# Sums of hi and lo parts for the token operands: VectorE instead of GpSimd

## The chip, the cores and the metric

The kernel runs on one core of a Trainium2 chip. The metric is the device time of one execution in microseconds (us), from the first to the last instruction and what lies around them; lower is better. The engines are TensorE (PE in the rows; PEld is its weight load), VectorE (DVE), ScalarE (ACT), GpSimd (POOL) and SyncE (SP), which issues nearly all DMA transfers here. Each engine takes its instructions strictly in the order in which they stand in its queue; semaphores order the engines among each other.

## The reference

One step of a diffusion backbone over 640 tokens (128 of a prompt, 512 samples) of 1024 features. The change touches the two feed-forward blocks that open and close the layer:

```python
def swiglu(h, w13, w2):
    a, b = jnp.split(h @ w13, 2, axis=-1)
    return (jax.nn.silu(a) * b) @ w2

def ffn_sublayer(x, norm_w, shift, scale, gate, w13, w2):
    return x + HALF_STEP * gate * swiglu(modulate(rms_norm(x, norm_w), shift, scale), w13, w2)
```

`w13` has 2 x 2816 columns, `w2` 2816 rows. Between the two blocks stand a gated delta-rule mixer and a windowed attention, which the change does not touch. All values are float32.

## The kernel before, in words

Tokens lie along the free axis, in two halves of 320 (`HT`); features lie on the partitions, in 8 tiles of 128 (`KD`). TensorE multiplies in a reduced format, so every operand is split exactly into a first part (hi) and a rest (lo), and a product takes three matmuls: hi x hi, hi x lo, lo x hi. For token operands the parts are the tiles `hh` and `hl`; for weights `wh`/`wl` (1024 columns) and `sh`/`sl` (512 columns, L128 on ScalarE and L132 on VectorE), made from `wraw`, which SyncE loads.

A feed-forward block (`ffn`) goes over 22 pairs of feature tiles f, in six rounds (`ROUNDS`); behind each round come its products with `w2`. The first three, f = 0, 1, 2 (`DIRECT`), are computed directly: a and b over all 8 k tiles, 48 matmuls each; then SiLU of a on ScalarE (L491), the multiplication with b on VectorE, which reads b from PSUM (L492, two instructions, one for each half), and the split of the result (L501 ScalarE, L502 VectorE). From f = 3 on `product_pair` computes a and b by seven products of quarters instead of eight, in the order p1, p6, p5, p7, two more into one large bank, p4, 12 matmuls each (L207). For these it needs differences of quarters of the weights, four GpSimd instructions (L577 to L580), and of the token operands.

The token operands of that kind are made once for each block, while TensorE does f = 1 and f = 2. `combined_operands` is called behind f = 1: for each of four k tiles (`KH`) it adds hi and lo of three quarters again (L536, GpSimd), takes three differences (L541, VectorE) and splits each (L544 ScalarE to `th`, L545 VectorE to `tl`). `last_operand` is called behind f = 2: for each of four tiles two such sums (L558, GpSimd), one difference (L562), and its split into the place of the quarter B12 of `hh`/`hl` (L563 ScalarE, L564 VectorE). This last operand, T4, is needed by p4 alone. So there are 12 + 8 sums in each block, 40 in the kernel.

What sets the order of the work: a tile scheduler puts each engine's instructions in a queue by its own estimates of when they are ready; the code's order is only its starting point. PSUM tiles called `aux` are four banks used in turn: a product of f = 2 takes the banks that the L492 of f = 1 and the modulation copies have to free, and p6 and p5 take those that the L492 of f = 2 frees. There are three `wraw` buffers, so a load of weights waits until the parts of an earlier one are made. In the first block the quarters of the modulation vectors are also computed in between (L277 load `araw` by SyncE, L281 TensorE, L290 and L292 VectorE).

```python
if f == 1:
    B = self.combined_operands(hs)
if f == DIRECT - 1:
    self.last_operand(hs, B)
```

Of the kernel before, what the change touches and what calls it, by code (L numbers as in the profile page):

```python
# [10 lines left out]
F32 = mybir.dt.float32  # L11
# [4 lines left out]
ALU = mybir.AluOpType  # L16
PSUM = bass.MemoryType.PSUM
DRAM = bass.MemoryType.DRAM
# [6 lines left out]
T = SEQ + DEC  # L25
# [70 lines left out]
# columns of a half (0: the prompt and the first 192 samples, 1: samples alone) by kind, 0 prompt, 1 sample  # L96
# [3 lines left out]
class Net:  # L100
# [9 lines left out]
    # ---------------------------------------------------------------- weights  # L110
# [8 lines left out]
    def parts(self, raw, small=False):  # L119
        """Exact split of float32 weights into two float32r parts."""  # L120
        nc = self.nc
        n = raw.shape[1]
        if small:
            hi, lo = (self.tile(self.phase, [P, n], F32R, tag, self.nsh) for tag in ("sh", "sl"))
        else:
            hi, lo = (self.tile(self.wpool, [P, KD * P], F32R, tag, self.nwh)[:, :n] for tag in ("wh", "wl"))
        with self.tc.high_priority(offset=0 if self.first_weights else 20):
            nc.scalar.copy(hi, raw)  # L128
            if self.first_weights:
                nc.gpsimd.tensor_tensor(lo, raw, hi.bitcast(F32), op=ALU.subtract)  # L130
            else:
                nc.vector.tensor_sub(lo, raw, hi.bitcast(F32))  # L132
        return hi, lo
# [10 lines left out]
    def product(self, w, xs, c0=0, split=None):  # L144
        """[128 features, tokens] = w^T x over the k tiles; operands come as exact parts. split: None for one
        view of both halves, otherwise a view of each half, in small tiles when true."""
        if split:
            hv = [self.aux_tile()[:, 0:HT] for _ in range(2)]
        else:
            ps = self.tile(self.big, [P, 2, 512], F32, "big", 2)  # L150
            hv = (ps[:, 0, 0:HT], ps[:, 1, 0:HT])
        if self.by_half:
            self.by_half -= 1
            self.accumulate(hv, w, xs, c0, (1,))
            self.accumulate(hv, w, xs, c0, (0,))
        else:
            self.accumulate(hv, w, xs, c0, (0, 1))
        return ps[:, :, 0:HT] if split is None else hv
# [26 lines left out]
    def products_by_half(self, ws, xs, done):  # L185
        """Several products with the second halves of all before the first ones; done(i, half, psum)."""
        for h in (1, 0):
            for i, w in enumerate(ws):
                if h:
                    ps = self.aux_tile()[:, 0:HT]  # L190
                else:
                    if i % 2 == 0:
                        both = self.tile(self.big, [P, 2, 512], F32, "big", 2)
                    ps = both[:, i % 2, 0:HT]
                self.accumulate({h: ps}, w, xs, 0, (h,))
                if h == 0 and i == len(ws) - 1:
                    yield
                done(i, h, ps)

    def products(self, ps, w, xs):  # L200
        """One half of the tokens and of the k tiles: ps (+)= w^T x."""
        nc = self.nc
        wh, wl = w
        n = len(xs)
        for k, (xh, xl) in enumerate(xs):
            for j, (wt, xt) in enumerate(((wh, xh), (wh, xl), (wl, xh))):
                nc.tensor.matmul(  # L207
                    ps,
                    lhsT=wt[:, k * P : (k + 1) * P],
                    rhs=xt,  # L210
                    start=(k == 0 and j == 0),
                    stop=(k == n - 1 and j == 2),
                )

    # ---------------------------------------------------------------- small helpers
    def rsqrt(self, y, x):
        """y = x ** -0.5, elementwise on a small tile."""
# [14 lines left out]
    # ---------------------------------------------------------------- setup  # L232
# [37 lines left out]
    def modulation(self, m):  # L270
        """One of the nine modulation vectors, features on partitions, for prompt and sample; a generator with one
        quarter of the k tiles in each step."""
# [34 lines left out]
    def modulation_part(self, m0, g):  # L307
        """Two feature tiles (2 g, 2 g + 1) of the modulation vectors m0 and m0 + 1."""
# [35 lines left out]
    def scale_columns(self, m, at, t, d0=0, n=KD):  # L344
        """norm weight * (1 + scale) as per-partition columns."""
# [9 lines left out]
    def token_rstd(self, ss):  # L355
        """[128 tokens, n] sums of squares -> rstd."""
# [8 lines left out]
    def half_rstd(self, acc, h):  # L365
        """rstd of the tokens of one half, from squares [128, 2, 320]: columns of 128 tokens that start at 0, 128
        and 192, so the last one overlaps."""
# [8 lines left out]
    def half_rows(self, columns):  # L376
        """(column of 128 tokens, first token, tokens, place) -> a row [320] on each partition."""
# [19 lines left out]
    def modulated(self, hs, X, rb, A, m_shift, h, ds):  # L397
        """x * rstd * A + shift of one half as two exact parts, for the feature tiles ds."""
# [23 lines left out]
    def next_operands(self, last, X, A, m_shift):  # L422
        """Operands of the next products; last: the generator that makes the last tiles of X."""
# [14 lines left out]
    def add_square(self, acc, x, first):  # L438
        """acc (+)= x * x for one half."""
# [15 lines left out]
    def residual(self, ws, xs, X, gate, tail, weight=None):  # L455
        """X += gate * product, with the squares of the sums gathered in acc; the last tiles go by halves."""
# [18 lines left out]
    # ---------------------------------------------------------------- ffn  # L475
    def ffn(self, hs, X, gate, w13, w2, gpool, between=None, first=(), weight=None):
        """X += gate * swiglu(h); squares of the result are gathered into acc."""
# [49 lines left out]
    def combined_operands(self, hs):  # L527
        """The parts of the sums of quarters of h = [[B11, B12], [B21, B22]] (k halves by token halves) that
        product_pair takes: T1 = B12 - B11, T2 = B22 - T1, T3 = B22 - B12."""
        nc = self.nc  # L530
        T = [[], [], []]
        for d in range(KH):
            v = []
            for k, h in ((d, 1), (d, 0), (d + KH, 1)):
                t = self.tile(self.phase, [P, HT], F32, "ht", self.nht)
                nc.gpsimd.tensor_tensor(t, *(x[:, h, :].bitcast(F32) for x in hs[k]), op=ALU.add)  # L536
# [13 lines left out]
    def last_operand(self, hs, B):  # L550
        """B21 - T2, in the place of B12."""
        nc = self.nc
        B["T4"] = []
        for d in range(KH):
            v = []
            for x in (B["21"][d], B["T2"][d]):
                t = self.tile(self.phase, [P, HT], F32, "ht", self.nht)
                nc.gpsimd.tensor_tensor(t, x[0].bitcast(F32), x[1].bitcast(F32), op=ALU.add)  # L558
# [8 lines left out]
    def product_pair(self, w, ca, cb, B, s):  # L567
        """s = silu(a) * b for the products a, b of two tiles of features with h, by seven products of quarters
        in place of eight (Winograd's form of Strassen's product)."""
# [42 lines left out]
    # ---------------------------------------------------------------- attention  # L612
    def rope(self, x, pool):
        """Rotates x [128 = 2 heads, samples] in place."""
# [9 lines left out]
    def attention_inputs(self, pool, tmp, hs):  # L624
        """Parts of the keys (columns: prompt, cache, samples, cache again), values with tokens on partitions,
        queries."""
# [57 lines left out]
    def query_parts(self, pool, qall, c, r):  # L684
        """Exact parts of the queries of one r and of blocks c and c + 1: for each head of the two, the first
        part on its own partitions and the second on the other head's."""
# [16 lines left out]
    def attention_block(self, pool, c, kd, kl, vt, qall):  # L703
        """One block of 128 queries; a generator, so that blocks can be interleaved."""
# [75 lines left out]
    # ---------------------------------------------------------------- mixer A inputs  # L780
# [69 lines left out]
    def conv(self, pool, ps, tile_index, out):  # L850
        """Centred short convolution and silu of one 128-channel tile; out [128, 640]."""
# [25 lines left out]
    def to_token_major(self, src, dst):  # L877
        """src [128, 640] -> dst[:, c, :]."""
# [8 lines left out]
    def mixer_a_inputs(self, tmp):  # L887
        """Generators, one for each head and kind, that make the inputs of the delta rule."""
# [47 lines left out]
    def feed(self, primary, late, units, hs, rounds):  # L936
        """Products of the units spread over the rounds of another generator, each followed by its unit's own
        work, in pieces."""
# [40 lines left out]
    # ---------------------------------------------------------------- delta rule  # L979
    def delta_front(self, pool, scan_pool, c, units):  # L980
        """L, I + L and the intra-chunk weights of both directions of one chunk."""
# [54 lines left out]
    def delta_prep(self, pool, scan_pool, c, units):  # L1036
        """(I + L)^-T of both directions of one chunk."""
# [50 lines left out]
    def delta_step(self, pool, c, dr, units, S, zero, update, first):  # L1088
        """One chunk of the scan; S [128 dk, 4, 128 dv] is updated in place."""
# [61 lines left out]
    def interleave(self, active, pending, width):  # L1151
        """Emits generators round robin, `width` at a time; a generator may start more."""
# [70 lines left out]
    def delta_output(self, pool, c):  # L1223
        """o * rstd * onorm * silu(z) of a finished chunk, in the place of o; the query's own norm enters
        through eps alone."""
# [30 lines left out]
    def z_gate(self, pool, h, ps):  # L1256
        """silu(z) * onorm of one head, kept in DRAM until the end of the scan."""
# [9 lines left out]
    def after(self, k):  # L1267
        """Where step k of a product has its place: behind the modulation parts at the start, spread over the
        products of the delta rule while it runs."""
# [20 lines left out]
    def operand(self, z, tiles):  # L1290
        """Exact split of z [128, 2, 320] into two float32r parts, in the tiles given."""
# [92 lines left out]
    def output(self, pool, X, acc):  # L1384
        """Final norm, back to tokens on partitions; X comes with the weight of the norm in it."""
# [22 lines left out]
    # ---------------------------------------------------------------- everything  # L1408
    def build(self):
# [12 lines left out]
        with (  # L1422
# [8 lines left out]
            # first half step  # L1431
# [57 lines left out]
            # mixer  # L1489
            with ExitStack() as right:  # L1490
# [67 lines left out]
                with pool("x2") as xpool:  # L1558
# [11 lines left out]
                    # second half step  # L1570
# [40 lines left out]
```

## Time and profile before

| | |
|---|---|
| median of 3 runs | 1606.71 us (1606.54 to 1610.02) |
| span of the profiled execution | 1605.0 us |
| instructions | 28532 |
| TensorE busy | 1542.7 us, 96% |
| VectorE busy | 1100.8 us, 69% |
| ScalarE busy | 664.5 us, 41% |
| GpSimd busy | 368.7 us, 23% |
| chain that ended last, by engine | TensorE 80%, VectorE 11%, issue 3%, ScalarE, DMA and GpSimd 2% each |

The profile is of one execution and lists no separate time for it: its span stands beside the runs' times, 1.7 us under their median. Busy time is the share in which an engine works at all; it is an average over stages. The chain that ended last is followed back from the last instruction, at each step to what released it. "issue" is time in which an engine waited for nothing that the profile shows. Idle time of an engine costs something only where TensorE, or whatever ends last, waits for it.

### The profile page before, as it was taken

Reading aid. Unit: us, or ns where it says so; the run is one execution under the profiler, and the core shown is the slowest. Engines: PE = TensorE matmul, PEld = TensorE weight load, DVE = VectorE, ACT = ScalarE, POOL = GpSimd, SP = SyncE. Lnnn points to the kernel's source line nnn. Section 1 sums busy time; section 2 is a strip of 40 time slices with the busy share of each in tenths; the row PEclk is TensorE's granted clock in tenths of the full one; section 3 lists DMA queues with packets and bytes.
Section 4 is the critical chain, followed back from the end, with each engine's and each line's share of the span. In section 5 each row is a group of like instructions: output and inputs, shape, how many; then the busy total and the mean of one; then the engine's idle time right before and its main releaser. Section 6 shows DMA issues by size and latency. Waiting matters only on the chain.

```text
span 1605.0 us, 28532 instructions
## 1 busy us (share of the span) xinstructions
PE 1542.7 (96%) x11242; PEld 1457.5 (91%) x11242; DVE 1100.8 (69%) x2241; ACT 664.5 (41%) x1234; POOL 368.7 (23%) x306
## 2 busy tenths in 40 slices
PE   6989999999999899999899999999879999999998
PEld 4889999999999798788899999899879999999997
DVE  5866666668576768886665655764796766767675
ACT  4433323324243646554455544333542424334244
POOL 3632131222220220100221213000352232331310
PEclk8999999999999999999999999999999999999999
DMA  9444434545325241214533324545022322323122
GB/s 329 148 144 141 159 123 143 163 152 168 119 82 137 82 138 44 65 40 134 161 117 94 98 78 127 158 127 167 14 79 79 92 66 66 106 66 106 53 79 66
DMA packets 221296, 181.17 MB, mean 113 GB/s; under 512 B 16160, under 2 KB 198621, under 8 KB 221163
## 3 DMA queue, kind: packets, MB, share of 16 engines
q1 hardware_dynamic: 220907, 179.29, 36.3%
q8 instruction: 89, 1.46, 0.4%
q14 instruction: 44, 0.36, 0.1%
q0 software_dynamic: 256, 0.06, 0.0%
HBM read 161.59 MB, written 16.42 MB: 111 GB/s over the span
## 4 chain that ended last, share of the span: by engine, by line
PE 80%; DVE 11%; issue 3%; ACT 2%; DMA 2%; POOL 2%; SPq 0%; POOLq 0%; DVEq 0%; ACTq 0%
PE big L177 29%; PE aux L207 20%; PE aux L177 9%; PE aux L164 9%; PE big L207 8%; DVE ht L404 1%; DVE wl L132 1%; PE aux L281 1%; DVE ht L541 1%; DVE sl L132 1%; PE aux L161 1%; DMA wraw<-ffn_w 1%; DVE x L451 1%; DVE tl L545 1%; DVE cacc L867 1%
## 5 line engine op out<-in xcount | busy, mean ns | idle before, releaser
L128 ACT CAST wh<-wraw 128x1024 fp32r<-128x1024 f32 (+1 forms) x147 | 150.8, 1026 | 266.3 <-PE aux L177 90.1
L132 DVE TENSOR_TENSOR wl<-wraw,wh 128x1024 fp32r<-128x1024 f32 (+1 forms) x145 | 181.8, 1254 | 85.7 <-ACT wh L128 84.4
L177 PE MATMUL big<-hl,wh 128*128 128x320 f32 x768 | 194.7, 321 | 6.9 <-POOL hl L411 4.3
L177 PE MATMUL big<-hh,wh 128*128 128x320 f32 x768 | 187.8, 319 | 4.0 <-ACT hh L1293 1.8
L177 PE MATMUL big<-hh,wl 128*128 128x320 f32 x768 | 187.8, 315 | 0.7 <-DVE wl L132 0.7
L128 ACT CAST sh<-ss 128x512 fp32r<-128x512 f32 x152 | 92.5, 620 | 185.1 <-POOL ss L578 93.6
L577 POOL TENSOR_TENSOR ss<-wraw 128x512 f32<-128x512 f32 x38 | 53.9, 1418 | 485.0 <-DMA wraw<-ffn_w 337.3
L132 DVE TENSOR_TENSOR sl<-ss,sh 128x512 fp32r<-128x512 f32 x152 | 132.3, 880 | 46.8 <-ACT sh L128 45.9
L207 PE MATMUL aux<-th,sh 128*128 128x320 f32 x456 | 141.3, 310 | 3.2 <-DVE s L492 2.8
L177 PEld LDWEIGHTS big<-hl,wh 128*128 128x128 f32 x768 | 131.4, 190 | 13.0 <-POOL hl L411 7.0
L207 PE MATMUL aux<-tl,sh 128*128 128x320 f32 x456 | 141.1, 309 | 0.0
L207 PE MATMUL aux<-th,sl 128*128 128x320 f32 x456 | 140.8, 309 | 0.0
L177 PEld LDWEIGHTS big<-hh,wh 128*128 128x128 f32 x768 | 129.0, 190 | 9.8 <-issue 3.1
L177 PEld LDWEIGHTS big<-hh,wl 128*128 128x128 f32 x768 | 131.1, 190 | 5.8 <-issue 4.6
L451 DVE SCALAR_TENSOR_TENSOR x<-big,gate,x 128x128 f32<-128x128 f32 (+2 forms) x181 | 67.4, 422 | 34.6 <-PE big L177 34.3
L177 PE MATMUL big<-gh,wh 128*128 128x320 f32 x352 | 88.7, 313 | 1.1 <-ACT gh L501 1.1
L207 PEld LDWEIGHTS aux<-th,sh 128*128 128x128 f32 x456 | 85.8, 188 | 4.0 <-DVE s L492 3.0
L177 PE MATMUL big<-gl,wh 128*128 128x320 f32 x352 | 87.6, 310 | 0.0
L177 PE MATMUL big<-gh,wl 128*128 128x320 f32 x352 | 87.0, 308 | 0.0
L207 PEld LDWEIGHTS aux<-tl,sh 128*128 128x128 f32 x456 | 85.7, 188 | 0.0
L207 PEld LDWEIGHTS aux<-th,sl 128*128 128x128 f32 x456 | 85.7, 188 | 0.0
L1055 DVE TENSOR_TENSOR P<-aux,lv 128x512 f16<-128x512 f32 x70 | 48.2, 688 | 49.1 <-PE aux L164 49.1
(373 smaller groups left out, 4014.0 us busy)
## 6 DMA issues: line engine op xcount, KB each, us to landing
wraw<-ffn_w SPq DMA_DIRECT2D x116, 512.0 KB, 3.9
araw<-ada_w SPq DMA_DIRECT2D x56, 512.0 KB, 5.8
wraw<-w_in SPq DMA_DIRECT2D x35, 512.0 KB, 3.8
araw<-ada_w SPq DMA_DIRECT2D x32, 256.0 KB, 6.5
wraw<-ffn_w SPq DMA_DIRECT2D x16, 384.0 KB, 3.1
gd<-stage SPq DMA_DIRECT2D x16, 320.0 KB, 2.9
wraw<-w_out SPq DMA_DIRECT2D x8, 512.0 KB, 4.3
xd<-x SPq DMA_DIRECT2D x8, 320.0 KB, 2.2
```

What stands on the lines that cost most here:

```text
L128: nc.scalar.copy(hi, raw)
L132: nc.vector.tensor_sub(lo, raw, hi.bitcast(F32))
L161: self.marks.append(self.nc.tensor.transpose(*args))
L164: self.marks.append(self.nc.tensor.matmul(*args, **kw))
L177: self.nc.tensor.matmul(ps[h], lhsT=wt[:, k, c0 : c0 + P], rhs=xt[:, h, :], start=(k == 0 and j == 0), stop=(k == len(xs) - 1 and j == 2),)
L207: nc.tensor.matmul(ps, lhsT=wt[:, k * P : (k + 1) * P], rhs=xt, start=(k == 0 and j == 0), stop=(k == n - 1 and j == 2),)
L281: nc.tensor.matmul(ps[32 * g : 32 * g + 32], lhsT=self.s32[:, k, :], rhs=raw[:, g * 256 : (g + 1) * 256], start=(k % 2 == 0), stop=(k % 2 ...
L404: mark = nc.vector.scalar_tensor_tensor(t[:, cols], X[d][:, h, cols], A[:, d, v : v + 1], rb[:, cols], op0=ALU.mult, op1=ALU.mult)
L451: nc.vector.scalar_tensor_tensor(X[:, h, cols], ps[:, cols], gate[:, d, v : v + 1], X[:, h, cols], op0=ALU.mult, op1=ALU.add)
L541: nc.vector.tensor_sub(f[i], v[x], v[y] if y < 3 else f[0])
L577: nc.gpsimd.tensor_tensor(f[0], b[:, :n], b[:, n:], op=ALU.add)
L1055: nc.vector.tensor_tensor(P16, p1, mask, op=ALU.mult)
```

## The change

The engine of two instructions changes; what they compute and which tiles they read and write stays. (Comments and docstrings were also dropped, without moving a line.)

```diff
@@ combined_operands
             for k, h in ((d, 1), (d, 0), (d + KH, 1)):
                 t = self.tile(self.phase, [P, HT], F32, "ht", self.nht)
-                nc.gpsimd.tensor_tensor(t, *(x[:, h, :].bitcast(F32) for x in hs[k]), op=ALU.add)
+                nc.vector.tensor_tensor(t, *(x[:, h, :].bitcast(F32) for x in hs[k]), op=ALU.add)
                 v.append(t)
@@ last_operand
             for x in (B["21"][d], B["T2"][d]):
                 t = self.tile(self.phase, [P, HT], F32, "ht", self.nht)
-                nc.gpsimd.tensor_tensor(t, x[0].bitcast(F32), x[1].bitcast(F32), op=ALU.add)
+                nc.vector.tensor_tensor(t, x[0].bitcast(F32), x[1].bitcast(F32), op=ALU.add)
                 v.append(t)
```

TensorE's order stays the same. 40 instructions leave GpSimd's queue and 40 enter VectorE's, and the scheduler arranges VectorE's and ScalarE's around them anew. In SyncE's queue one modulation load now stands ahead of one weight load (`wraw_1058`, the second weights of f = 3) in the first block.

VectorE's queue in the first block, between the operands of `combined_operands` and the multiplication L492 of f = 1 (`s_655`; `aux_718` and `aux_717` are the banks of its product b). Before:

```order
L545 TENSOR_TENSOR tl_864<-ht_851,th_863 128x320
L562 TENSOR_TENSOR ht_1007<-ht_1003,ht_1005 128x320
L132 TENSOR_TENSOR sl_1073<-ss_1061,sh_1072 128x512
L562 TENSOR_TENSOR ht_1015<-ht_1011,ht_1013 128x320
L132 TENSOR_TENSOR sl_1077<-ss_1060,sh_1076 128x512
L562 TENSOR_TENSOR ht_1023<-ht_1019,ht_1021 128x320
L132 TENSOR_TENSOR sl_1081<-ss_1062,sh_1080 128x512
L132 TENSOR_TENSOR sl_1085<-ss_1063,sh_1084 128x512
L492 TENSOR_TENSOR s_655<-s_655,aux_718 128x320
L492 TENSOR_TENSOR s_655<-s_655,aux_717 128x320
```

With the change:

```order
L545 TENSOR_TENSOR tl_864<-ht_851,th_863 128x320
L132 TENSOR_TENSOR wl_946<-wraw_943,wh_945 128x1024
L492 TENSOR_TENSOR s_655<-s_655,aux_718 128x320
L492 TENSOR_TENSOR s_655<-s_655,aux_717 128x320
L292 TENSOR_TENSOR modr_624<-modr_624,aux_873 128x256
L502 TENSOR_TENSOR gl_654<-s_655,gh_653 128x320 x2
L558 TENSOR_TENSOR ht_1003<-hh_217,hl_218 128x320
L558 TENSOR_TENSOR ht_1005<-th_787,tl_788 128x320
L132 TENSOR_TENSOR wl_1069<-wraw_1056,wh_1068 128x1024
L562 TENSOR_TENSOR ht_1007<-ht_1003,ht_1005 128x320
```

The multiplication stood behind three differences of `last_operand` (L562) and four parts of the f = 3 weights (`sl`); now it stands right behind the last operand of `combined_operands` and one weight part of f = 2, and the work of `last_operand` comes behind it.

VectorE's queue in the second block, around the last two weight parts of f = 2 (`wl_13524` of a, `wl_13579` of b) and the multiplication of f = 1 (`s_13302`), as the piece of the difference:

```order
 L545 TENSOR_TENSOR tl_13479<-ht_13472,th_13478 128x320
-L132 TENSOR_TENSOR wl_13579<-wraw_13576,wh_13578 128x1024
+L132 TENSOR_TENSOR wl_13524<-wraw_13521,wh_13523 128x1024
 L545 TENSOR_TENSOR tl_13483<-ht_13476,th_13482 128x320
 L545 TENSOR_TENSOR tl_13487<-ht_13474,th_13486 128x320
+L492 TENSOR_TENSOR s_13302<-s_13302,aux_13365 128x320
+L492 TENSOR_TENSOR s_13302<-s_13302,aux_13364 128x320
+L536 TENSOR_TENSOR ht_13490<-hh_12510,hl_12511 128x320
+L536 TENSOR_TENSOR ht_13492<-hh_12510,hl_12511 128x320
```

Each of the two weight parts has moved back: `wl_13579` from the third of the four k tiles of `combined_operands` to behind the fourth. It is out of the piece here, further down:

```order
 L545 TENSOR_TENSOR tl_13507<-ht_13500,th_13506 128x320
 L545 TENSOR_TENSOR tl_13511<-ht_13498,th_13510 128x320
-L502 TENSOR_TENSOR gl_13301<-s_13302,gh_13300 128x320 x2
+L502 TENSOR_TENSOR gl_13301<-s_13302,gh_13300 128x320
+L132 TENSOR_TENSOR wl_13579<-wraw_13576,wh_13578 128x1024
+L558 TENSOR_TENSOR ht_13636<-hh_12512,hl_12513 128x320
+L558 TENSOR_TENSOR ht_13638<-th_13434,tl_13435 128x320
+L132 TENSOR_TENSOR wl_13688<-wraw_13675,wh_13687 128x1024
 L562 TENSOR_TENSOR ht_13640<-ht_13636,ht_13638 128x320
```

All 12 sums of `combined_operands` now stand ahead of it, and the first two of `last_operand` right behind it.

## Rows read from the trace of the kernel before

**Rows 1.** The page: the span, and busy us, share of it and instructions of each engine.

```profile
span 1605.0 us, 28532 instructions
...
PE 1542.7 (96%) x11242; PEld 1457.5 (91%) x11242; DVE 1100.8 (69%) x2241; ACT 664.5 (41%) x1234; POOL 368.7 (23%) x306
```

**Rows 2.** Windows: length, busy us (instructions) by engine, TensorE clock granted, DMA share, GB/s.

```profile
105.00:300.00 195.00, 193.47 (x1430) 182.34 (x1430) 124.62 (x235) 61.01 (x94) 49.29 (x37) 1.00 0.45 144
83.00:89.00 6.00, 0.20 (x2) 0.00 (x0) 5.25 (x8) 0.26 (x1) 4.97 (x5) 0.89 0.03 13
89.00:94.40 5.40, 5.32 (x20) 5.32 (x21) 5.40 (x11) 3.67 (x8) 0.35 (x1) 0.50 0.34 105
1187.60:1193.50 5.90, 0.61 (x3) 0.30 (x2) 5.90 (x8) 3.74 (x7) 3.55 (x3) 0.71 0.01 1
1193.50:1197.00 3.50, 3.48 (x13) 3.48 (x14) 3.50 (x6) 0.62 (x2) 1.42 (x2) 0.51 0.47 150
1198.50:1201.30 2.80, 0.05 (x2) 0.01 (x1) 2.62 (x7) 1.43 (x3) 0.12 (x1) 1.00 0.79 252
```

**Rows 3.** TensorE in order of time: start, us, line, operation, xcount, [idle before, what ended it].

```profile
62.08 0.64 PE L281 MATMUL aux<-araw,s 128*32 128x256 f32 x8 [1.55 <-DMA araw<-ada_w]
...
89.08 0.64 PE L177 MATMUL aux<-hh,wh 128*128 128x320 f32 x1 [5.88 <-DVE s L492]
...
1180.74 0.46 PE L177 MATMUL aux<-hl,wh 128*128 128x320 f32 x2
1181.04 0.46 PE L177 MATMUL aux<-hh,wl 128*128 128x320 f32 x2
...
1188.40 0.41 PE L207 MATMUL aux<-hh,wh 128*128 128x320 f32 x1 [0.75 <-ACT wh L128]
...
1193.52 0.63 PE L207 MATMUL aux<-hh,wl 128*128 128x320 f32 x1 [4.56 <-DVE wl L132]
...
1201.30 0.42 PE L207 MATMUL aux<-th,sh 128*128 128x320 f32 x1 [2.75 <-DVE s L492]
```

**Rows 4.** Groups of GpSimd instructions, both stages: busy us, mean ns, idle us before and releasers.

```profile
L536 POOL TENSOR_TENSOR ht<-hh,hl 128x320 f32<-128x320 f32 x24 | 28.7, 1220 | 10.4 <-DVE ht L541 10.4
```

**Rows 5.** Groups of VectorE instructions, columns as in 4: 1159.9 to 1201.5, then 50.7 to 98.4 us.

```profile
L541 DVE TENSOR_TENSOR ht<-ht,ht 128x320 f32<-128x320 f32 x12 | 11.2, 981 | 1.6 <-POOL ht L536 1.6
L545 DVE TENSOR_TENSOR tl<-ht,th 128x320 fp32r<-128x320 f32 x12 | 9.6, 816 | 0.0
...
L562 DVE TENSOR_TENSOR ht<-ht,ht 128x320 f32<-128x320 f32 x4 | 1.9, 479 | 0.0
...
L545 DVE TENSOR_TENSOR tl<-ht,th 128x320 fp32r<-128x320 f32 x12 | 10.8, 931 | 0.1
L541 DVE TENSOR_TENSOR ht<-ht,ht 128x320 f32<-128x320 f32 x12 | 9.4, 830 | 2.9 <-POOL ht L536 2.9
```

**Rows 6.** VectorE in order of time, columns as in 3.

```profile
48.89 1.76 DVE L416 SCALAR_TENSOR_TENSOR hl<-ht,mod,hh 128x128 fp32r<-128x128 f32 x3
...
61.67 1.28 DVE L541 TENSOR_TENSOR ht<-ht,ht 128x320 f32<-128x320 f32 x3
...
63.28 1.21 DVE L132 TENSOR_TENSOR wl<-wraw,wh 128x1024 fp32r<-128x1024 f32 x1
64.42 0.88 DVE L545 TENSOR_TENSOR tl<-ht,th 128x320 fp32r<-128x320 f32 x2
...
1157.86 0.78 DVE L416 SCALAR_TENSOR_TENSOR hl<-ht,mod,hh 128x192 fp32r<-128x192 f32 x1 [0.26 <-ACT hh L414]
...
1179.92 4.59 DVE L541 TENSOR_TENSOR ht<-ht,ht 128x320 f32<-128x320 f32 x3
...
1195.67 0.68 DVE L132 TENSOR_TENSOR sl<-wraw,sh 128x512 fp32r<-128x512 f32 x1
```

**Rows 7.** GpSimd in order of time: the first subtraction of product_pair in stage 2.

```profile
1178.26 1.39 POOL L577 TENSOR_TENSOR ss<-wraw 128x512 f32<-128x512 f32 x1 [1.25 <-issue]
```

**Rows 8.** ScalarE in order of time, stage 1.

```profile
52.77 1.05 ACT L128 CAST wh<-wraw 128x1024 fp32r<-128x1024 f32 x1 [1.48 <-PE big L177]
```

## The prediction

> **What bounds the kernel now.** Read the busy shares first. TensorE is busy for 1542.7 of 1605.0 us [rows 1], so a change off TensorE can only give back TensorE's pauses. The span of this one execution stands 1.7 us under the median of the runs, 1606.71; I work in the span and add the 1.7 back at the end. VectorE is busy 69% and GpSimd 23%, which says nothing yet about the two short stretches that the change touches.
>
> Then the table of windows [rows 2]. From 105 to 300 us TensorE misses only 1.5 of 195 us: a steady stage, with nothing to win. The two feed-forward starts are different. [...]
>
> Then TensorE's own order of time [rows 3], for what ended each pause. Stage 1 (first feed-forward): 5.88 us until VectorE's L492. Stage 2 (second): 0.75, 4.56 and 2.75 us, ended by a ScalarE copy, VectorE's L132 and VectorE's L492. All these VectorE instructions were late because of their place in a full queue, not because of long work of their own. The L492 multiplications free the PSUM banks of a finished product.
>
> **The price of what TensorE loses.** A 320-column matmul starts every 0.147 us at full clock (two in 0.29 to 0.30 us, the spacing of the rows at 1180.74 and 1181.04 [rows 3]) and every 0.267 us at the low one (20 in 5.32, 13 in 3.48 [rows 2]). Stage 1 therefore loses 5.9 + 20 x 0.12 = 8.3 us, and stage 2 8.06 + 13 x 0.12 = 9.6 us.
>
> **What is removed.** In each stage 20 GpSimd sums go, 12 of L536 at 1.22 us and 8 of L558 [rows 4], nearly all the GpSimd work there. While GpSimd works, VectorE is slow: L541 and L545 average 0.98 and 0.82 us in stage 2, 0.83 and 0.93 in stage 1 [rows 5]. The same L541 in a gap of GpSimd goes three in 1.28 us, that is 0.43 each [rows 6]. Beside the four GpSimd subtractions of product_pair, the first at 1178.26 [rows 7], three of them take 4.59 us [rows 6]: one VectorE instruction in the 1.53 us of a GpSimd one. Against 0.48 us for one alone (L562 [rows 5]), the 24 instructions of L541 and L545 carry 10.0 us of excess in stage 2 and 9.6 us in stage 1.
>
> **What is added.** VectorE gets 20 additions per stage of the form, operand types and size of L541. I take 0.43 us: 8.6 us per stage. The bounds are 0.40 (two independent L545 take 0.88 and one takes 0.48, so the second starts 0.40 after the first) and 0.98, the mean under GpSimd [rows 5, 6]. I stand near the low end because the GpSimd work that makes the high end is the work that leaves. [...]
>
> **Stage 1, counted.** VectorE's last operand instruction ends at 50.65 [rows 6]. From there to the first L492 of f=2 the new order holds 61 instructions of 128x320 (52 of L536 to L564, 9 of L492 and L502), 6 weight parts of 1024 columns at 1.14 us (63.28 to 64.42), 5 of 512 at 0.61 (0.68 less the same overlap of 0.07) and 3 modulation copies, at 0.40 each: 26.2 + 6.8 + 3.1 + 1.2 = 37.3 us. Waits: 0.8 us for ScalarE's copy of the f=1 weights, which ends at 53.82 [rows 8]; about 1.1 us at L292, which waits for modulation matmuls near 64.2 us, with L545 instructions queued behind it; and the four subtractions, under which four VectorE instructions worth about 2.1 us take 4 x 1.53, so some 4.0. Sum: 93.9 us.
>
> TensorE first runs on where it stood. L492 of f=1 now stands ahead of the eight L558, near 76 us, so its bank is free before 83. The modulation load also lands about 0.4 us earlier (SyncE issues it behind a weight load that waits for a VectorE part), which shortens the 1.55 us pause at 62 [rows 3]. So the second product of f=2 starts near 82.5, its 48 matmuls take 7.05, modulation 1.1, p1 1.76: 92.4, where p6 needs the bank of that L492. By this count a wait of 1.5 us is left. I left out the hand-overs between engines, which only lengthen it, and take 2.0. **Stage 1 gains 8.3 + 0.4 - 2.0 = 6.7 us.** A wait of 2.0 leaves the clock alone: the pause of 4.56 us was followed by 0.51, that of 2.75 by matmuls at full pace [rows 2, 3].
>
> **Stage 2, counted.** VectorE is free from 1158.64 [rows 6]. The part wl_13579 of the f=2 weights now stands behind all 12 L536: 44 instructions at 0.43 and 3 weight parts at 1.14 end at 1181.0; 0.3 us of wait for SiLU and 0.7 where a weight part meets a subtraction make it 1182.0. TensorE wants it at 1181.04 [rows 3]: a new wait of 1.0 us. From there to the L492 of f=2, whose bank p5 needs, are 9 x 0.43 + 1.14 + 5 x 0.61 = 8.1 us, and 3.3 more under the other three subtractions: 1193.4. TensorE, without any wait, would come to p5 at 1187.65 + 24 x 0.147 = 1191.2. So 2.2 us of waiting are left in all, at L132, at L492 or shared, and I take 2.5. Behind it in VectorE's queue stand 12 more instructions until T4 is complete, near 1198.6; p4 starts near 1200.4, a cover of 1.8 us. **Stage 2 gains 9.6 - 2.5 = 7.1 us.**
>
> At no cost: the order of the loads (one modulation load passes one weight load that waits for wl_891 anyway), that weight load's later landing (near 76, its parts are needed at 92), ScalarE's new order (busy 41% [rows 1]), and GpSimd, whose remaining subtractions have no sums ahead of them.
>
> **Sum.** 6.7 + 7.1 = 13.8 us: a span of 1591.2, a time of 1592.9.
>
> **Rivals.**
>
> *All comes back.* The leftover waits vanish, because sums without dependence go at 0.40 and the subtractions fall beside ScalarE's work. 8.7 + 9.6 = 18.3 us: 1588.4.
>
> *The leftovers reach the clock.* If each 128x320 instruction of the counts takes 0.48 from start to start, the waits are 1.5 + 3.0 = 4.5 and 2.2 + 2.7 = 4.9 us, and the clock falls after each as it does now (2.4 and 1.6 us). Gains 1.8 and 3.1: 1601.8. For it: the queue ahead of the late instruction is full in both stages. Against: 0.43 us is measured.
>
> *Nothing moves.* The new waits are as long as the old ones, within 3.2 us of 1606.7. For it: in both stages a weight part or an L492 still stands behind all the sums. Against: the excess of 10 us is over the 8.6 added, and L492 of f=1 passes eight sums.
>
> *VectorE becomes the bound.* If VectorE's slowness there is not GpSimd's doing but comes from all engines working on the same operands, nothing of the excess goes, and the sums add at least 20 x 0.40 = 8.0 us per stage to the queue ahead of L132 and L492: 1622.7. It decides as soon as less than 8 of the 10 us goes with the GpSimd sums. Against: the three L541 at 0.43 [rows 6] ran with TensorE and ScalarE at work and GpSimd idle.
>
> **Chances.** Forecast 0.50, all back 0.14, leftovers with low clock 0.21, nothing 0.09, slower 0.06. No change means within 0.2% (3.2 us), about what a measurement can tell. The first three are faster: 0.85; same 0.09; slower 0.06. The range takes in the first three, 1587.5 to 1602.5.
>
> **What would show it.** Right: L541 and L545 near 0.45 us; no pause at 83 us; a pause of 1 to 3 us near 92 us until L492, and one near 1181 us until L132, with the granted clock at 1.00 behind both; none at 1188 us. Wrong: L541 still near 0.9 us with GpSimd empty, low clock behind a new pause, or the 14 us lost again between 105 and 1130 us to waits for loads.

## The result, and the profile after

| | before | changed |
|---|---|---|
| median, first comparison (4 runs each) | 1608.24 us (1606.54 to 1610.02) | 1595.45 us (1593.51 to 1597.29) |
| ratio, 95% interval | | 0.9921 (0.9902 to 0.9940) |
| median, compared again later (E8; 17 and 6 runs) | 1606.78 us (1601.99 to 1612.36) | 1598.19 us (1594.43 to 1600.07) |
| ratio, 95% interval | | 0.9944 (0.9926 to 0.9961) |
| span of the profiled execution | 1605.0 us | 1592.7 us |

The change makes the kernel faster, by 0.6% in the later comparison and 0.8% in the first. One of the seven executions of E4 below took 8426.77 us; it counts in E4's median there, and not in its ratio. The page of the changed kernel, the span and the busy time of each engine (answers to [rows 1]):

```profile
span 1592.7 us, 28513 instructions
...
PE 1540.9 (97%) x11242; PEld 1455.9 (91%) x11242; DVE 1091.1 (69%) x2281; ACT 664.6 (42%) x1234; POOL 327.0 (21%) x266
```

VectorE has 40 instructions more and is busy 9.7 us less. The sums came, and more than their price went. Groups of VectorE instructions in stage 2, 1150 to 1196 us (answers to [rows 5]; stage 1 has 484 and 486 ns for L541 and L545):

```profile
L545 DVE TENSOR_TENSOR tl<-ht,th 128x320 fp32r<-128x320 f32 x12 | 5.4, 486 | 0.0
L536 DVE TENSOR_TENSOR ht<-hh,hl 128x320 f32<-128x320 f32 x12 | 5.3, 484 | 0.0
L541 DVE TENSOR_TENSOR ht<-ht,ht 128x320 f32<-128x320 f32 x12 | 5.3, 484 | 0.0
```

L541 fell from 0.98 to 0.48 us, L545 from 0.82 to 0.49.

TensorE in order of time, the rows with a wait in the two stages (answers to [rows 3]; stage 2 begins some 8 us earlier than before):

```profile
61.14 0.64 PE L281 MATMUL aux<-araw,s 128*32 128x256 f32 x8 [0.99 <-DMA araw<-ada_w]
...
93.56 0.39 PE L207 MATMUL aux<-th,sh 128*128 128x320 f32 x1 [1.46 <-DVE s L492]
...
1183.78 0.41 PE L207 MATMUL aux<-th,sl 128*128 128x320 f32 x1 [2.10 <-DVE sl L132]
...
1187.48 0.39 PE L207 MATMUL aux<-th,sh 128*128 128x320 f32 x1 [1.97 <-DVE s L492]
...
1199.38 0.42 PE L177 MATMUL big<-gh,wh 128*128 128x320 f32 x1 [1.26 <-ACT gh L501]
```

The 5.88 us at 83 and the 4.56 us for a weight part are gone. What is left stands at other places, and the windows around it (answer to [rows 2]) have the granted clock at 1.00:

```profile
91.00:96.00 5.00, 3.54 (x25) 3.31 (x24) 5.00 (x9) 2.30 (x5) 0.00 (x0) 1.00 0.60 194
1176.00:1190.00 14.00, 9.93 (x66) 9.44 (x65) 7.37 (x16) 7.91 (x15) 4.33 (x4) 1.00 0.23 76
```

So stage 1 won 5.88 + 2.4 (low clock) + 0.56 (the load at 61) - 1.46 = 7.4 us, stage 2 9.6 - 2.10 - 1.97 - 1.26 = 4.3 us: 11.7 of the 12.3 us by which the span is shorter.

Why are there pauses in stage 2 at all? GpSimd in order of time shows something new: the first subtraction of product_pair, 1.39 us before [rows 7], now lasts 4.28 and 6.00 us.

```profile
76.41 4.28 POOL L577 TENSOR_TENSOR ss<-wraw 128x512 f32<-128x512 f32 x1 [25.39 <-DMA wraw<-ffn_w]
...
1170.53 6.00 POOL L577 TENSOR_TENSOR ss<-wraw 128x512 f32<-128x512 f32 x1 [20.11 <-DMA wraw<-ffn_w]
1176.61 1.30 POOL L578 TENSOR_TENSOR ss<-ss,wraw 128x512 f32<-128x512 f32 x1
```

VectorE in order of time, around the same places:

```profile
79.05 0.48 DVE L558 TENSOR_TENSOR ht<-th,tl 128x320 f32<-128x320 f32 x1
82.75 1.12 DVE L132 TENSOR_TENSOR sl<-ss,sh 128x512 fp32r<-128x512 f32 x1 [3.22 <-ACT sh L128]
...
1174.89 0.49 DVE L558 TENSOR_TENSOR ht<-th,tl 128x320 f32<-128x320 f32 x1
1182.63 0.49 DVE L564 TENSOR_TENSOR hl<-ht,hh 128x320 fp32r<-128x320 f32 x1 [7.25 <-ACT hh L563]
```

In both stages L577 ends 1.15 us behind the end of VectorE's last instruction (79.53 to 80.69; 1175.38 to 1176.53), and the next subtraction, alone, takes 1.30: it seems to have done its work only when VectorE stopped, which E9 tests. Then VectorE stood idle for 3.22 and 7.25 us, since ScalarE's next copies are those of the subtractions' results, with the copies of last_operand (L563) queued behind them. ScalarE in stage 2:

```profile
1177.94 1.87 ACT L128 CAST sh<-ss 128x512 fp32r<-128x512 f32 x3 [7.95 <-POOL ss L578]
...
1182.14 0.46 ACT L563 CAST hh<-ht 128x320 fp32r<-128x320 f32 x1
```

From here two things were to be told apart. **Theory A:** GpSimd at work in SBUF slows VectorE, whoever waits for it, and the change wins by taking that work away. **Theory B:** on top of that, VectorE without a gap keeps GpSimd out, and this cost part of the win. Rivals: the order of VectorE's queue alone, or waits of VectorE for GpSimd's results.

### The profile page after: what moved, and what is told of

Same layout as the page of the kernel before. It is cut to its first block, busy times and chain, and to the rows that moved or that the text cites. A ratio compares the mean times of both kernels' runs of the same rounds, so it can differ in the third digit from the quotient of the medians.

```text
span 1592.7 us, 28513 instructions
## 1 busy us (share of the span) xinstructions
PE 1540.9 (97%) x11242; PEld 1455.9 (91%) x11242; DVE 1091.1 (69%) x2281; ACT 664.6 (42%) x1234; POOL 327.0 (21%) x266
## 3 DMA queue, kind: packets, MB, share of 16 engines
q8 instruction: 89, 1.46, 0.4%
## 4 chain that ended last, share of the span: by engine, by line
PE 80%; DVE 10%; ACT 3%; DMA 3%; issue 2%; POOL 2%; SPq 0%; POOLq 0%; ACTq 0%; DVEq 0%
PE big L177 30%; PE aux L207 20%; PE aux L164 9%; PE aux L177 9%; PE big L207 8%; DMA wraw<-ffn_w 1%; PE aux L281 1%; DVE wl L132 1%; POOL ss L577 1%; DVE sl L132 1%; DVE ht L404 1%; DVE x L451 1%; PE aux L161 1%; ACT wh L128 1%; DVE cacc L867 1%
## 5 line engine op out<-in xcount | busy, mean ns | idle before, releaser
L577 POOL TENSOR_TENSOR ss<-wraw 128x512 f32<-128x512 f32 x38 | 60.2, 1583 | 528.0 <-DMA wraw<-ffn_w 356.5
L451 DVE SCALAR_TENSOR_TENSOR x<-big,gate,x 128x128 f32<-128x128 f32 (+2 forms) x181 | 67.5, 423 | 34.3 <-PE big L177 34.0
```

Source lines behind the costliest of these rows:

```text
L451: nc.vector.scalar_tensor_tensor(X[:, h, cols], ps[:, cols], gate[:, d, v : v + 1], X[:, h, cols], op0=ALU.mult, op1=ALU.add)
L577: nc.gpsimd.tensor_tensor(f[0], b[:, :n], b[:, n:], op=ALU.add)
```

## The experiments

The runs of E1 to E4 share one set of runs of before, those of E5 to E8 another, and those of E9 to E11 a third (medians 1607.21, 1606.78, 1607.08 us).

| | median us | ratio to before, 95% interval |
|---|---|---|
| E1 combined_operands only | 1601.01 | 0.9952 (0.9935 to 0.9968) |
| E2 last_operand only | 1599.86 | 0.9950 (0.9935 to 0.9964) |
| E3 change, first pairs' subtractions too | 1587.96 | 0.9881 (0.9859 to 0.9904) |
| E4 first pairs' subtractions only | 1601.56 | 0.9960 (0.9942 to 0.9978) |
| E6 change, idle GpSimd sums | 1602.99 | 0.9979 (0.9965 to 0.9992) |
| E7 change, all subtractions | 1587.21 | 0.9873 (0.9850 to 0.9896) |
| E8 the change again | 1598.19 | 0.9944 (0.9926 to 0.9961) |
| E10 the change in the second block only | 1601.51 | 0.9965 (0.9953 to 0.9978) |
| E11 E7 without GpSimd's operand parts | 1583.53 | 0.9854 (0.9835 to 0.9873) |

### E1, E2: half of the change each

E1 puts L558 back on GpSimd, E2 in the same way L536:

```diff
-                nc.vector.tensor_tensor(t, x[0].bitcast(F32), x[1].bitcast(F32), op=ALU.add)
+                nc.gpsimd.tensor_tensor(t, x[0].bitcast(F32), x[1].bitcast(F32), op=ALU.add)
```

> Only the 12 sums of combined_operands (L536) are on VectorE; the 8 of last_operand (L558) stay on GpSimd. VectorE's queue keeps the new place of the multiplication L492 of f = 1, ahead of last_operand. Theory A (each engine is slowed while the other works in SBUF): the first half of each stage is as fast as in the change (L541 and L545 at 0.48 us, no pause at 83 us), the second half as slow as before (L562 and sl near 1.1 us), so pauses of 3 to 5 us near 92 us and in stage 2: 1597 to 1601 us. Rival B (VectorE in an unbroken run keeps GpSimd out, and the late pieces are what the first four GpSimd subtractions L577 to L580 deliver): with eight instructions fewer VectorE's run breaks early, L577 is done in under 2 us, and it is as fast as the change or faster: 1591 to 1595 us.

> Only the 8 sums of last_operand (L558) are on VectorE; the 12 of combined_operands (L536) stay on GpSimd. Theory A: L541 and L545 stay at 0.8 to 1.0 us, the pause at 83 us shrinks from 5.9 to 1 to 3 us since GpSimd is empty behind the subtractions, stage 2 gains little because its weight part still waits behind slow sums: 1600 to 1604 us. Rival (it is the place of L492 in the queue alone, not the speed of VectorE, that the change improves): L492 of f = 1 stands behind six instructions of last_operand, so the pause of stage 1 stays and nothing is won: 1606 to 1610 us.

E1, 1601.01 us: GpSimd, then TensorE in order of time, then a window behind its pause.

```profile
71.86 4.39 POOL L558 TENSOR_TENSOR ht<-hh,hl 128x320 f32<-128x320 f32 x1 [20.36 <-DVE ht L541]
```

```profile
1196.04 0.61 PE L207 MATMUL aux<-th,sh 128*128 128x320 f32 x1 [6.36 <-DVE s L492]
```

```profile
1194.00:1200.00 6.00, 3.96 (x15) 3.99 (x16) 5.90 (x12) 3.05 (x6) 0.00 (x0) 0.50 0.61 178
```

The first half is fast as A says, the second slow, with pauses of 3.2 us in stage 1 and 6.4 us in stage 2, longer than A's 5, at the upper edge of A's time. B's expectation of 1591 to 1595 fell, for GpSimd's eight sums queue up with the subtractions. But the first of them is held out for 4.39 us, as B has it.

E2, 1599.86 us: VectorE's groups from 47 to 95 us, then TensorE in stage 2.

```profile
L541 DVE TENSOR_TENSOR ht<-ht,ht 128x320 f32<-128x320 f32 x12 | 10.5, 922 | 1.9 <-POOL ht L536 1.9
L545 DVE TENSOR_TENSOR tl<-ht,th 128x320 fp32r<-128x320 f32 x12 | 7.9, 692 | 0.1
```

```profile
1183.21 0.41 PE L207 MATMUL aux<-hh,wl 128*128 128x320 f32 x1 [3.44 <-DVE wl L132]
...
1190.57 0.41 PE L207 MATMUL aux<-th,sh 128*128 128x320 f32 x1 [2.34 <-DVE s L492]
```

L541 stays slow while L536 runs on GpSimd, and stage 2 keeps its late weight part. Stage 1 has no pause at 83 at all, better than A's 1 to 3 us, though L492 of f = 1 stands behind six instructions of last_operand. So it does not take the new place of L492, ahead of last_operand; it is enough that GpSimd's work near it is gone.

### E3, E4: the four subtractions of the first pair

E3 is the change with this; E4 has the same with both sums on GpSimd:

```diff
@@ product_pair
-    def product_pair(self, w, ca, cb, B, s):
+    def product_pair(self, w, ca, cb, B, s, engine):
...
-            nc.gpsimd.tensor_tensor(f[0], b[:, :n], b[:, n:], op=ALU.add)
+            engine.tensor_tensor(f[0], b[:, :n], b[:, n:], op=ALU.add)
@@ ffn
-                    self.product_pair(w13, f * P, D_FF + f * P, B, s)
+                    self.product_pair(w13, f * P, D_FF + f * P, B, s, nc.vector if f == DIRECT else nc.gpsimd)
```

> The change, and the four GpSimd subtractions of the first product_pair of each block (L577 to L580) on VectorE too, so GpSimd has nothing to do in the two stages. Theory B (in the changed kernel the first of these takes 4.28 and 6.00 us because VectorE runs without a gap, VectorE then idles 3.2 and 7.3 us for its results, and that makes the pauses of 1.46, 2.10 and 1.97 us): VectorE gets 4 x 0.60 = 2.4 us per stage in the place of this idle time, and 3 to 5.5 us more are won than by the change: 1590 to 1592.5 us, pauses under 0.7 us. Rival (VectorE is simply full there): 2.4 us more work per stage make the pauses longer, 1598 to 1601 us.

> All 20 sums per stage back on GpSimd; only the four subtractions of the first product_pair of each block go to VectorE. Theory A: the sums still slow L541 and L545 (0.8 to 1.0 us while L536 runs); some 4 us of slowness beside the subtractions go and 2.4 us of work come: 1603 to 1608 us. Rival (the subtractions, not the sums, were what cost before): at or under the time of the change, 1590 to 1597 us.

E3, 1587.96 us. VectorE's group in stage 1:

```profile
L577 DVE TENSOR_TENSOR ss<-wraw 128x512 f32<-128x512 f32 x1 | 0.7, 684 | 0.0
```

Between 82 and 110 and between 1160 and 1215 us TensorE has no wait that the profile lists: the pauses of 1.46, 2.10, 1.97 and 1.26 us are all gone, with 2.4 us more on VectorE in each stage. B is right on what the leftover pauses hung on, and VectorE is not full. The time is 2 us under the range expected, and its runs lie wide apart (1584.7 to 1593.9). The profiled execution, at 1593.53 us, is one of the long ones: its span is only 1.3 us under that of the change. TensorE waits 2.34 us for the modulation load there, the clock granted from 64 to 68 us is 0.57, and the first block's first L451, which adds its result to the tokens, comes at 115.1 us, against 112.9 in the change. In E7, which differs from E3 only in later pairs, that wait is 2.57 us, the granted clock behind it 1.00, and L451 comes at 108.4. So a part of the spread arises at this one load; whether it explains all of it is not shown.

E4, 1601.56 us, lies between the two expectations. Stage 1 wins most (1.28 us are left of the 5.88, and 0.44 at a later L492), stage 2 little. VectorE's group from 47 to 95 us, and TensorE in stage 2:

```profile
L541 DVE TENSOR_TENSOR ht<-ht,ht 128x320 f32<-128x320 f32 x12 | 7.2, 647 | 2.9 <-POOL ht L536 2.9
```

```profile
1190.85 0.61 PE L207 MATMUL aux<-th,sh 128*128 128x320 f32 x1 [6.23 <-ACT wh L128]
```

In stage 1 four GpSimd instructions fewer do most of what twenty fewer do. Counted from GpSimd's first sum, since E4's stage begins 3.3 us earlier (at 48.00 instead of 51.34 us), GpSimd is through after 33.7 us instead of 38.0, and L492 comes after 32.9 instead of 37.2. So the work that GpSimd has ahead of the bank counts there, of either kind. That the sums cost nothing of their own does not follow: L541 still takes 0.65 us. In stage 2 the subtractions do not suffice.

### E6, E8: GpSimd busy for nobody

E6 adds sums on GpSimd that nobody reads; E8 is the changed kernel itself.

```diff
@@ combined_operands; in ffn: self.second = not between
-                nc.vector.tensor_tensor(t, *(x[:, h, :].bitcast(F32) for x in hs[k]), op=ALU.add)
+                nc.vector.tensor_tensor(t, *(x[:, h, :].bitcast(F32) for x in hs[k]), op=ALU.add); self.second and nc.gpsimd.tensor_tensor(self.tile(self.phase, [P, HT], F32, "idle"), *(x[:, h, :].bitcast(F32) for x in hs[k]), op=ALU.add)
```

> The change, and in the second block GpSimd computes the 12 sums of combined_operands once more into a tile that nobody reads: GpSimd is busy as before the change, and no VectorE instruction waits for it. If GpSimd's work by itself slows VectorE (theory A), L541 and L545 in stage 2 go back to 0.8 to 1.0 us and the pauses of stage 2 to 6 to 9 us: 1599 to 1603 us. If an unbroken VectorE run keeps GpSimd out (theory B), L541 stays near 0.5 us, single idle sums last 2 us and more, and only the four subtractions behind them come later: 1596 to 1600 us. Rival (the change helps because VectorE no longer waits for GpSimd's results): the time of the change, 1594 to 1597 us, with L541 at 0.48 and the subtractions no later.

> The changed kernel itself, on the chip of the other three runs: 1593 to 1598 us, with the pauses of 1.46, 2.10 and 1.97 us at the same instructions.

E6, 1602.99 us, 4.8 us above E8. GpSimd's idle sums; VectorE's group L541 while they run (1154.3 to 1168.2) and behind them (to 1184); TensorE's pause; a window behind it:

```profile
1154.36 13.82 POOL L536 TENSOR_TENSOR idle<-hh,hl 128x320 f32<-128x320 f32 x12
```

```profile
L541 DVE TENSOR_TENSOR ht<-ht,ht 128x320 f32<-128x320 f32 x3 | 2.8, 938 | 0.0
...
L541 DVE TENSOR_TENSOR ht<-ht,ht 128x320 f32<-128x320 f32 x9 | 3.8, 476 | 0.0
```

```profile
1177.35 0.90 PE L177 MATMUL big<-hh,wl 128*128 128x320 f32 x2 [6.94 <-DVE wl L132]
```

```profile
1176.00:1182.00 6.00, 4.65 (x17) 4.65 (x18) 6.00 (x14) 2.56 (x6) 0.00 (x0) 0.50 0.33 91
```

No instruction waits for these sums, and yet L541 doubles while they run and falls back when they end, and a late weight part and the low clock return. That shows the cause: it is GpSimd's work beside VectorE's, not a wait for its results. VectorE's queue is not quite that of the change: the late weight part stands three instructions further back (one L536, two L545), some 1.2 us of the 6.94. The two rows of L541 do not depend on that. Here GpSimd began 0.2 us ahead of VectorE's sums, and the two took turns; B's version (VectorE undisturbed) did not show.

E8, 1598.19 us, just above the time expected, has the same pauses as the first profile of the change (1.5; 2.1, 2.0, 1.3 us), but 2.93 us at the modulation load of stage 1, where that had 0.99, and a low clock behind it:

```profile
62.86 0.98 PE L281 MATMUL aux<-araw,s 128*32 128x256 f32 x8 [2.93 <-DMA araw<-ada_w]
```

```profile
62.00:66.00 4.00, 3.14 (x16) 2.29 (x16) 0.12 (x1) 0.17 (x1) 0.00 (x0) 0.63 0.34 73
```

The first block's first L451 comes at 121.3 us before, at 112.9 in the first profile of the change and at 116.4 here. Two executions of one kernel differ by that much through this load, so its 0.56 us in the sum of stage 1 is no effect of the change that can be relied on, and of the 8.4 us at L451 E8 keeps 4.9.

### E5, E9: the two engines by themselves

Two pieces behind the kernel's end, each 128x320 sums on both engines. Each kernel ran once, 1632.52 us (E5) and 1677.99 us (E9); what counts are the rows.

> The changed kernel, and behind its last instruction a piece of its own that adds 128x320 tiles on VectorE and GpSimd in five stretches: VectorE alone (8 sums); GpSimd alone (4); GpSimd arriving with 2 sums in an unbroken run of VectorE; VectorE arriving with 6 sums in a run of GpSimd; the unbroken run again with one operand of VectorE in PSUM; and the run with a break in which VectorE waits for a ScalarE copy. Theory B (one of the two engines at a time reads and writes SBUF in such sums; an unbroken VectorE run is not interrupted): 0.40 us from start to start alone, GpSimd 0.88; in the unbroken run GpSimd's first sum lasts 3.5 us or more, until the run ends, and VectorE stays at 0.40; arriving second, VectorE goes one sum per GpSimd sum, 0.9 to 1.2 us; with the operand in PSUM both are as fast as alone; at the break GpSimd gets in. Rival (they share, each slowed whenever both work): GpSimd's sums last 1.2 to 1.8 us and VectorE's 0.6 to 0.9 us in every stretch with both. The whole is some 40 us longer than the change.

E5: GpSimd in order of time, the five rows in the order of arrival: alone, then with VectorE, VectorE arriving second, VectorE with a PSUM operand, the run with the break; then VectorE's rows of the third and fourth.

```profile
1596.77 3.42 POOL L1423 TENSOR_TENSOR pr<-pr,pr 128x320 f32<-128x320 f32 x4 [68.71 <-DVE pr L1423]
1601.32 2.23 POOL L1423 TENSOR_TENSOR pr<-pr,pr 128x320 f32<-128x320 f32 x2 [1.13 <-DVE pr L1423]
1608.59 4.22 POOL L1423 TENSOR_TENSOR pr<-pr,pr 128x320 f32<-128x320 f32 x4 [5.05 <-DVE pr L1423]
1615.62 1.68 POOL L1423 TENSOR_TENSOR pr<-pr,pr 128x320 f32<-128x320 f32 x2 [2.81 <-DVE pr L1423]
1622.04 2.22 POOL L1423 TENSOR_TENSOR pr<-pr,pr 128x320 f32<-128x320 f32 x2 [4.74 <-DVE pr L1423]
```

```profile
1609.48 5.08 DVE L1423 TENSOR_TENSOR pr<-pr,pr 128x320 f32<-128x320 f32 x7 [0.97 <-POOL pr L1423]
...
1615.06 5.78 DVE L1423 TENSOR_TENSOR pr<-pr,aux 128x320 f32<-128x320 f32 x14 [0.49 <-ACT aux L1451]
```

Alone GpSimd needs 0.86 us for a sum (four in 3.42), and 1.1 beside VectorE, which then goes one sum per GpSimd sum, three of the seven at 1.07 us. With one VectorE operand in PSUM both run as if alone: 0.84 us, and 14 sums at 0.41. So they take turns, as A has it, and sharing falls. B's unbroken run fell here: GpSimd, arriving as VectorE began its third sum, was let in at once. For the same reason the break tested nothing.

> The changed kernel with another piece behind its end. GpSimd's sums arrive in VectorE runs: after 12 sums of an unbroken run with 24 more to come; after 13 with 24 to come (three GpSimd sums); after 12 of a chain in which each sum reads the one before (0.53 us from start to start) with 12 to come; after 3 with 12 to come; after 24 with 24 to come. Theory B' (a run that has gone on for some sums is not interrupted, as in the changed kernel, where L577 lasts 4.28 and 6.00 us; a run that has just begun is, as in the first probe): the first GpSimd sum of the first, second and last stretch lasts 9 us and more, that of the third and fourth 1.2 us. Rival (arrival always alternates, and L577 was held up by something else): 1.2 us in all five, VectorE 1.1 us beside it.

E9: GpSimd in order of time, the five arrivals, and VectorE's run beside the first.

```profile
1600.72 10.20 POOL L1423 TENSOR_TENSOR pr<-pr,pr 128x320 f32<-128x320 f32 x1 [70.48 <-DVE pr L1423]
1616.96 11.83 POOL L1423 TENSOR_TENSOR pr<-pr,pr 128x320 f32<-128x320 f32 x3 [6.05 <-DVE pr L1423]
1635.71 3.29 POOL L1423 TENSOR_TENSOR pr<-pr,pr 128x320 f32<-128x320 f32 x3 [6.92 <-DVE pr L1423]
1645.57 3.17 POOL L1423 TENSOR_TENSOR pr<-pr,pr 128x320 f32<-128x320 f32 x3 [6.57 <-DVE pr L1423]
1662.75 11.92 POOL L1423 TENSOR_TENSOR pr<-pr,pr 128x320 f32<-128x320 f32 x3 [14.01 <-DVE pr L1423]
```

```profile
1600.47 9.33 DVE L1423 TENSOR_TENSOR pv<-pr,pr 128x320 f32<-128x320 f32 x23
```

Theory B' holds in all five. Behind 12, 13 or 24 sums without a gap, one GpSimd sum lasts 10.2 us or so: VectorE does its 23 sums at 0.40 us as if alone, and GpSimd is done 0.7 us after the run. Behind three sums, or in a chain that leaves a gap after every sum, GpSimd goes in turns. That is what L577 met in both stages of the changed kernel.

### E7, E10, E11: more of it, and less

E7 is the change with all of L577 to L580 on VectorE:

```diff
@@ product_pair
-            nc.gpsimd.tensor_tensor(f[0], b[:, :n], b[:, n:], op=ALU.add)
+            nc.vector.tensor_tensor(f[0], b[:, :n], b[:, n:], op=ALU.add)
...
```

E11 is E7 with the operand tiles of GpSimd (L411) made like the others:

```diff
-POOL_TILES = (1, 3, 4, 6)
+POOL_TILES = ()
```

E10 has the change at L536 and L558 in the second block alone:

```diff
@@ ffn
-        first = list(first)
+        first, self.sums = list(first), nc.vector if not between else nc.gpsimd
@@ last_operand, and the same in combined_operands
-                nc.vector.tensor_tensor(t, x[0].bitcast(F32), x[1].bitcast(F32), op=ALU.add)
+                self.sums.tensor_tensor(t, x[0].bitcast(F32), x[1].bitcast(F32), op=ALU.add)
```

> The change, and the four subtractions of every product_pair (38 of them, 152 instructions) on VectorE. VectorE gets 152 x 0.60 = 91 us more, GpSimd loses some 210 us. If the steady stages have room for it (VectorE 66% busy from 105 to 300 us): as fast as with the first pair of each block alone or faster, 1584 to 1590 us. Rival: the longer queue delays the weight parts of the steady stages by more than 0.2 us per pair, 1592 to 1600 us.

> The change in the second block alone; the first block as before. If the two stages count by themselves, stage 1 keeps its pause of 5.9 us and the low clock behind it, and only the 5.5 us that the trace shows for stage 2 are won: 1600 to 1603 us. Rival (what stage 1 wins is lost again later, or stage 2 wins nothing by itself): 1605 to 1608 us.

> All product_pair subtractions on VectorE, and the four of eight operand tiles whose lo part GpSimd makes (L411) go the way of the other four, over VectorE (L416). TensorE waits 4.3 us in all for these GpSimd parts in the changed kernel. If GpSimd's slowness makes these waits: 1583 to 1586 us. Rival (VectorE is what the operand stretches wait for; it already ends 2.3 us of waits there): the waits turn into waits for L416 and it is no faster than with the subtractions alone, 1587 to 1592 us.

E10, 1601.51 us, is 5.6 us under its before, as expected if the stages count by themselves. Stage 2 has the changed kernel's pauses of 2.1 and 2.0 us. Stage 1 keeps its pause until L492, 3.98 us here, behind a wait at the modulation load that is longer than before's 1.55 [rows 3] and has a low clock behind it:

```profile
61.54 0.64 PE L281 MATMUL aux<-araw,s 128*32 128x256 f32 x8 [1.97 <-DMA araw<-ada_w]
...
88.14 0.64 PE L177 MATMUL aux<-hh,wh 128*128 128x320 f32 x1 [3.98 <-DVE s L492]
```

```profile
62.00:66.00 4.00, 4.00 (x23) 2.75 (x20) 4.00 (x5) 0.82 (x2) 3.62 (x3) 0.57 0.46 136
```

E7, 1587.21 us, is faster than the change by 11.0 us in the same set of runs. Its page, and its window from 105 to 300 us:

```profile
PE 1537.7 (97%) x11242; PEld 1454.3 (92%) x11242; DVE 1146.7 (72%) x2433; ACT 665.7 (42%) x1234; POOL 110.3 (7%) x114
```

```profile
105.00:300.00 195.00, 195.00 (x1443) 184.19 (x1442) 145.30 (x280) 63.26 (x99) 0.00 (x0) 1.00 0.47 148
```

VectorE got 152 instructions of some 0.60 us, 91 us, and is busy 56 us longer: the rest is most likely what went with GpSimd's slowing. In the steady stage TensorE misses nothing of 195 us (1.5 before [rows 2]), so there is room.

E11, 1583.53 us, is the fastest of all, 1.5% under before; it lies 3.7 us below E7 in another set of runs, with intervals that overlap, so that this last step is likely and not shown.

## Why the prediction was right, and where it was off

**The forecast.** The range holds the result. The forecast of 1592.9 us is 2.6 us under the first median and 5.3 us under that of E8: a gain of 13.8 us was counted, and the two comparisons gave 12.8 and 8.6. The sign rested on stage 1 and on VectorE's excess, and both came; the size is in part luck, as the two stages show.

*The excess goes.* Right: "L541 and L545 near 0.45 us" measured 0.48 and 0.49, and E6 shows the cause apart from every wait.

*The price of a sum.* I took 0.43 us; the low bound of 0.40 was true (E9: 23 sums in 9.33 us). One sum by itself takes 0.48 us (L536, 484 ns); a queue of them counts by the 0.40 from start to start.

*Stage 1.* Predicted 6.7 us, measured 7.4 in the first profile, of which 0.56 us is the load's (0.4 was counted). L492 of f = 2 was to end its first half at 93.9 us and did at 93.4; the leftover was taken as 2.0 and is 1.46. The sum was right by luck, with errors inside it that nearly cancel: 61 instructions at 0.40 instead of 0.43 save 1.8 us, the subtractions slow VectorE by 1.5 us in the place of 4.0, and 3.22 us of idle time, which I did not have, take most of that back. *"A wait of 2.0 leaves the clock alone"* held for these pauses (1.46, 2.10 and 1.97 us, with the granted clock at 1.00 around them), but not as a rule: see the rivals.

*Stage 2.* Predicted 7.1 us, measured 4.3. **This is the step that failed:** "3.3 more under the other three subtractions" let GpSimd go on at 1.5 us each and VectorE take turns, as in [rows 6, 7]. The weight part `wl_13579` was in time, the wait of 1.0 us at it did not come. Instead VectorE's run held L577 out for 4.7 us, and the results of the subtractions became late: waits at `sl`, at L492 and at the copy behind them, 5.3 us where 2.5 were taken. The idle 7.25 us of VectorE behind it, until ScalarE's L563, stood under "At no cost", as ScalarE's new order and GpSimd's remaining subtractions. E3 takes the subtractions away and all of these go.

*Signs.* No pause at 83, one near 92 until L492, granted clock of 1.00: as said. The pause until `wl` near 1181 was not there; one of 2.10 us stands later, until an `sl`. "None at 1188 us" came true: the 0.75 and 4.56 us there are gone. The gain of stage 1 was not lost again; stage 2 begins 8 us earlier. So the 1.97 us until L492 at 1187.48 are no miss of that sign: they stand where 2.75 us stood at 1201.30 [rows 3], and the sum of stage 2 had left a wait there.

**The rivals.** *All comes back* is what E3 reaches with the subtractions moved too, 1588. *Nothing moves* fell with the old pauses. *The leftovers reach the clock* did not happen to the change's pauses of up to 2.10 us, and 0.40 us from start to start (E9) takes away its condition of 0.48. At the modulation load, though, 1.97 us in E10 was followed by 0.57, while 2.57 us there in E7, and the 2.75 us until L492 before the change [rows 3], were followed by a granted clock of 1.00 (before: from 1201.3 to 1206.3 us), so length alone does not say. *VectorE becomes the bound* fell with L541 at 0.48 us and with E6, which brings the slowness back by GpSimd's work alone; E7 adds 152 instructions on VectorE and is faster.

E5 shows turns of 1.07 us, and none when VectorE has an operand in PSUM (0.84 us for a GpSimd sum, 0.41 for one of VectorE). Turns are not all: in E9 a GpSimd sum lasted 10.2 us instead of 0.86, through the 24 VectorE sums that followed in the run.

## What to carry to other kernels

Price an instruction on GpSimd by what it does to VectorE too: here, in E5's turns of 1.07 us, each GpSimd sum cost VectorE about 0.7 us, more than the 0.40 us that VectorE needs to do it itself. When work leaves GpSimd, look at what stays there, because a VectorE that now runs without gaps can hold a remaining GpSimd instruction out for the length of its run (L577 lasted 6.00 us in stage 2 instead of 1.39); move that one too if others wait for its result. And count a queue by start to start, not by the length of one instruction (here 0.40 against 0.48 us).

## What the runs showed of the hardware that was not expected

GpSimd's sum of 0.86 us lasts some 10.2 us when it arrives behind 12, 13 or 24 sums of a VectorE run without a gap, and 1.1 us when it arrives after two or three (E5, E9). In E1 a run of seven held it out as well: the sum that arrived at 71.86 us ended at 76.25, 0.8 us after VectorE came to an L492 (75.43), which reads one operand from PSUM. What lies between three and seven was not tried, and why it is so stays open.
